# Twenty-six pairs that reorder the queues of VectorE, ScalarE and GpSimd in a two-layer hybrid encoder

## The chip, the cores and the metric

The kernel runs on one core of one Trainium2 chip. The metric is the device time of one launch in microseconds (us), as the median over several runs. Lower is better. TensorE does the matrix products, VectorE and ScalarE work on tiles in SBUF and PSUM, GpSimd works on SBUF, and SyncE's queue issues nearly all transfers.

## The reference: what is computed

Two layers, 512 grid tokens and 16 learned meta tokens, width 1024, all in float32. In short:

```python
for l in range(DEPTH):
    h = rms_norm(x, norm_g[l])
    qa, ka, va, ga, qn, kn, vn, gn, m_a, m_n = split_cols(h @ w_in[l])
    a = gqa_attention(rope(rms(qa)), rope(rms(ka)), va)      # 8 query heads, 2 key heads of 64
    b = neighbourhood_attention(rms(qn), rms(kn), vn, rpb)   # 8 heads, window 8 x 16, learned bias
    a = (a * silu(ga)) @ w_o_attn[l]
    b = (b * silu(gn)) @ w_o_na[l]
    x = x + (sigmoid(m_a) * a + sigmoid(m_n) * b) @ w_out[l]
out = rms_norm(x, final_norm_g)[:, N_META:]
```

## The kernel before, in words

Activations lie channel by channel: a tile has 128 channels as partitions and up to 528 tokens along the free axis. Every float32 product is made of three products of reduced-precision halves: `split` (line 196) writes the high half on ScalarE as a cast and the low half on VectorE as a subtraction, and a product is hi·hi, lo·hi and hi·lo (lines 327 to 329). A projection of 128 columns over 264 tokens is 24 matmuls of 128x264. Its tile is called `pp`, and in layer 0 it has two halves (`pp0_3_0`, `pp0_3_264`). For each 128x512 piece of weights, the `raw` load is followed by a cast `whi` on ScalarE (line 242) and a subtraction `wlo` on GpSimd (line 243), from rings of six buffers.

A name in an order is a tag with its layer, its head or column, and a serial number: `ptl1_2_1_2` is the low half `ptl`, layer 1, head pair 2, half 1, key tiles from 2 on.

- The grouped-query attention runs in units (layer, head pair, half): scores `S` (558, 559), an exponential into `P`, a 32x32 transpose on VectorE, a round trip through DRAM (`turn`, and the reads back at 879), the split into `pth` (ScalarE) and `ptl` (VectorE), and the sum with the values, `av` (907): two matmuls each for four key tiles, of which the ones with `ptl` can only start when the subtraction is done.
- The neighbourhood attention has, for each head, scores `Sb`, `bias` and exponentials (992, 994), transposes on TensorE into two shared PSUM banks (`ta`, `tm`, `tb`, `tc`, and `vtb`, `vtc` for the values), the splits `tah`, `tal`, `tbh`, `tbl`, `VB`, the meta part `na`, and the sum `avb` (1054).
- In layer 0 the norm of the input needs a row sum: the split `ssh`, `ssl` of the squares, and the small product `ms` (375). Beside it stand the products `mh` (474) that sum the squares of the queries and take `qh` and `ql`. `ql` is a subtraction (496) of `qs` and `qh`, which ScalarE writes when it empties a projection (492 to 494).
- The gates `zb`, `za` and `mg`, the branch outputs `oa`, `ob` with their splits, the merges `ma`, `mb`, `mx`, and a last product `pf` with the weights `wl` (1236 to 1238) fill the rest.

A scheduler puts the operations in order: it plans all engines together with costs of its own, gives split and softmax operations a higher priority, and keeps what `tc.issue_after` demands. Each engine then runs its queue strictly in order, and so does SyncE's DMA queue. So an operation that waits holds up all that stands behind it on its engine. `order only` dependencies on the same engine, as in this change, have no semaphore: they only make the scheduler put one behind the other, and it then plans all engines anew from there.

Of the kernel before, what the change touches and what calls it, by code (L numbers as in the profile page):

```python
# [58 lines left out]
BLK_PS = ((0, 0), (0, 208), (1, 0), (1, 272))  # L59

BLK_META = 448


def _window_index():
# [33 lines left out]
def trunk_kernel(ctx: ExitStack, tc: tile.TileContext, xT, w, gn, gf, bias, rope, out):  # L98
# [28 lines left out]
    def bank(pool, name, tag):  # L127
        return pool.tile([P, 512], F32, tag=tag, name=name)

    def transposed(ps, src, n=P):  # L130
        nc.tensor.transpose(ps, src, ident[:n, :n])
# [77 lines left out]
    order = []  # L209
    for l in range(DEPTH):  # L210
# [4 lines left out]
        if l == 0:  # L215

            order = order[6:]
# [238 lines left out]
    for l in range(DEPTH):  # L456
# [512 lines left out]
        def windowed_head(hd):  # L969
# [66 lines left out]
            def transposes3():  # L1036
                tp = bank(ps_t, f"tc{nm}", "tp")
                transposed(tp[:64, :P], c["bias"][:, BLK_META:BLK_META + 64])

# [115 lines left out]
        for m in range(8 + LAG_A):  # L1155
# [9 lines left out]
            if m >= LAG_A:  # L1165
# [3 lines left out]
                for a, b in merge_half(m - LAG_A, gates[m - LAG_A], WOA, oa, ma):  # L1169
                    if (end and full) or b == N:  # L1170
                        a = a if end else 0
# [52 lines left out]
    for f in range(2):  # L1224
        for t in range(4):
# [31 lines left out]
            else:  # L1257
# [6 lines left out]
                with tc.high_priority():  # L1264
# [2 lines left out]
                    nc.vector.tensor_scalar_mul(x, x, r)  # L1267
                    nc.sync.dma_start(out[P * t:P * (t + 1), 2 * h2:], x)
    side_gqa.finish()


# [45 lines left out]
```

## Time and profile before

| | |
|---|---|
| median of 3 runs | 836.88 us (836.46 to 838.2) |
| profiled execution | 837.78 us, of which the span of the trace is 834.8 us and 2.98 us lie around it |
| TensorE busy | 817.3 us, 98% of the span |
| VectorE, ScalarE, GpSimd busy | 522.5, 474.1 and 419.6 us (63, 57 and 50%) |
| chain that ended last | TensorE 81%, VectorE 6%, ScalarE 5%, DMA 4% |

The share of TensorE is so high that only the moments count in which it waits, or in which its clock is halved. The view of waits names the instruction that waits and the engine that ended the wait. In a row of the timeline the first number is the start in us from the start of the span, the second the duration, then engine, line, operation and tiles (without buffer numbers) and, in brackets, how long the engine was idle before and what ended that.

### The profile page before, as it was taken

To read this page: it belongs to the slowest core of one execution; us is meant where nothing else is said; L and a number is where in the kernel's file an instruction comes from. 1 tells how busy PE (TensorE), PEld (TensorE's weight loads), DVE (VectorE), ACT (ScalarE), POOL (GpSimd) and SP (SyncE) were. 2 spreads that over 40 slices of the span, in tenths; PEclk is the share of its full clock that TensorE was granted. 3 is DMA by queue.
4 is the path that set the end of the run, shared out by engine and by line. 5 is a ranking of instruction groups with operands and counts; after the bars stand their busy time and mean duration, and the time that the engine had idled before them with its cause. 6 is when DMAs were issued, how large, how long until landed. Compare 5 with 4: busy or idle time off the path is not lost.

```text
span 834.8 us, 16105 instructions
## 1 busy us (share of the span) xinstructions
PE 817.3 (98%) x5662; PEld 759.0 (91%) x5662; DVE 522.5 (63%) x1152; ACT 474.1 (57%) x1137; POOL 419.6 (50%) x362
## 2 busy tenths in 40 slices
PE   9899999999999999999999999999999999999997
PEld 9899999999999999999998989898898888888786
DVE  7876767677765573446448667676857755443633
ACT  8545677577865555434345457566847756443422
POOL 1654534545354444655764645453535464454751
PEclk9899999999999999999999999999999999999999
DMA  8357564766564564334655585546775555661502
GB/s 305 100 156 211 163 188 128 201 176 177 176 192 135 160 204 145 111 102 142 165 130 133 145 235 146 185 154 186 182 227 155 183 156 167 186 203 66 189 1 101
DMA packets 113248, 134.98 MB, mean 162 GB/s; under 512 B 31888, under 2 KB 66192, under 8 KB 113168
## 3 DMA queue, kind: packets, MB, share of 16 engines
q1 hardware_dynamic: 112448, 132.90, 53.6%
q8 instruction: 44, 0.72, 0.4%
q10 hardware_dynamic: 720, 1.06, 0.3%
q14 instruction: 36, 0.29, 0.1%
HBM read 98.50 MB, written 21.84 MB: 144 GB/s over the span
## 4 chain that ended last, share of the span: by engine, by line
PE 81%; DVE 6%; ACT 5%; DMA 4%; issue 2%; SPq 1%; POOLq 0%; POOL 0%; DVEq 0%; ACTq 0%
PE pp L329 17%; PE pp L327 17%; PE pp L328 17%; PE av L907 4%; PE y L329 4%; PE y L327 4%; PE y L328 4%; PE avb L1054 2%; PE S L558 2%; PE S L559 2%; PE pf L1238 2%; PE pf L1236 2%; PE pf L1237 2%; DMA turn<-P 1%; DVE ptl L196 1%
## 5 line engine op out<-in xcount | busy, mean ns | idle before, releaser
L243 POOL TENSOR_TENSOR wlo<-raw,whi 128x512 fp32r<-128x512 f32 x210 | 285.4, 1368 | 271.6 <-ACT whi L242 225.2
L327 PE MATMUL pp<-hh,whi 128*128 128x264 f32 (+3 forms) x1040 | 326.5, 314 | 0.0
L329 PE MATMUL pp<-hh,wlo 128*128 128x264 f32 (+3 forms) x1040 | 325.0, 312 | 0.0
L328 PE MATMUL pp<-hl,whi 128*128 128x264 f32 (+3 forms) x1040 | 324.2, 312 | 0.0
L329 PEld LDWEIGHTS pp<-hh,wlo 128*128 128x128 f32 x1040 | 196.7, 189 | 10.3
L328 PEld LDWEIGHTS pp<-hl,whi 128*128 128x128 f32 x1040 | 197.1, 190 | 9.3
L327 PEld LDWEIGHTS pp<-hh,whi 128*128 128x128 f32 x1040 | 196.4, 189 | 8.8
L242 ACT CAST whi<-raw 128x512 fp32r<-128x512 f32 x210 | 128.1, 619 | 133.4 <-PE pp L328 56.9
L900 POOL TENSOR_TENSOR ga<-pm,ga 32x128 fp32r<-32x128 f32 x64 | 41.2, 643 | 83.4 <-ACT ga L898 44.9
L869 DVE STREAM_TRANSPOSE P<-P 128x512 f32<-128x512 f32 x64 | 46.6, 728 | 32.3 <-ACT P L843 31.5
L196 DVE TENSOR_TENSOR ptl<-P,pth 128x512 fp32r<-128x512 f32 x64 | 56.3, 891 | 8.2 <-ACT pth L195 8.0
L1133 DVE TENSOR_TENSOR mg<-pp,rbc 128x264 f32<-128x264 f32 (+1 forms) x48 | 24.7, 514 | 47.9 <-PE pp L329 47.5
L839 DVE CUSTOM_DVE_ANT_1 P<-S,r 128x528 f32<-128x528 f32 x64 | 44.8, 700 | 13.9 <-PE S L559 12.9
L843 ACT ACTIVATE P<-P,st 128x528 f32<-128x528 f32 x64 | 47.1, 736 | 1.7
L994 ACT ACTIVATE bias<-bias,stb 128x208 f32<-128x208 f32 (+1 forms) x64 | 31.0, 486 | 22.2 <-DVE stb L992 22.1
L195 ACT CAST pth<-P 128x512 fp32r<-128x512 f32 x64 | 39.2, 613 | 2.7 <-DMA P<-turn 2.2
L1134 ACT ACTIVATE mg<-mg 128x264 f32<-128x264 f32 (+1 forms) x48 | 23.6, 492 | 27.5 <-DVE mg L1133 27.4
L907 PE MATMUL av<-ptl,VA 128*128 128x256 f32 x128 | 33.7, 291 | 3.0 <-DVE ptl L196 2.9
L328 PE MATMUL pp<-mx,whi 128*128 128x264 f32 x128 | 36.6, 286 | 0.0
L327 PE MATMUL pp<-mx,whi 128*128 128x264 f32 x128 | 36.4, 284 | 0.0
L329 PE MATMUL pp<-mx,wlo 128*128 128x264 f32 x128 | 36.3, 283 | 0.0
L907 PE MATMUL av<-pth,VA 128*128 128x256 f32 x128 | 34.2, 291 | 0.0
(534 smaller groups left out, 1704.4 us busy)
## 6 DMA issues: line engine op xcount, KB each, us to landing
raw<-in_w_dram SPq DMA_DIRECT2D x210, 256.0 KB
turn<-P SPq DMA_DIRECT2D x32, 528.0 KB
P<-turn SPq DMA_DIRECT2D x128, 128.0 KB
bias<-in_bias_dram SPq DMA_DIRECT2D x16, 480.0 KB
KB<-KB SPq DMA_DIRECT2D x24, 272.0 KB
rawl<-in_w_dram SPq DMA_DIRECT2D x16, 256.0 KB
x<-in_xT_dram SPq DMA_DIRECT2D x8, 264.0 KB
xr<-in_xT_dram SPq DMA_DIRECT2D x8, 264.0 KB
```

The costliest lines, as they stand in the source:

```text
L195: split_at["hi"] = nc.scalar.copy(hi, src)
L196: split_at["any"] = nc.vector.tensor_sub(lo, src, hi.bitcast(F32))
L242: cast = nc.scalar.copy(hi, raw)
L243: sub = nc.gpsimd.tensor_sub(lo, raw, hi.bitcast(F32))
L327: nc.tensor.matmul(ps, wh, rh[:, a:b], start=i == 0, stop=False)
L328: nc.tensor.matmul(ps, wh, rl[:, a:b], start=False, stop=False)
L329: nc.tensor.matmul(ps, wl, rh[:, a:b], start=False, stop=i == n - 1)
L839: newest["max"] = nc.vector.tensor_tensor_reduce(p[:n].rearrange("p (i k) -> p i k", i=2), S[:n, :, :HALF], scale[:n].unsqueeze(2).to_broa ...
L843: nc.scalar.activation(p[:n], p[:n], AF.Exp, bias=st[:n, 1:2], scale=1.0, accum_out=st[:n, 2:3] if total is None else total)
L869: nc.vector.transpose(c["both"][:n, a:b], c["both"][:n, a:b])
L900: nc.gpsimd.tensor_sub(tm[64 + 32 * t:96 + 32 * t, n * t:n * (t + 1)], m, tm[:32, :n].bitcast(F32))
L907: nc.tensor.matmul(c["av"], rows2(c["t"][i][0]), c["t"][i][1], start=i == 0, stop=i == 8)
```

## The change

A table of pairs and a function that is called once, after all operations are recorded. In a pair `(a, n, b, m)`, the n-th operation that writes tile `a` gets an order-only dependency on the m-th one that writes `b`, on the same engine. No operation is added, removed or changed: on all five queues the same instructions stand, in another order. One pair (`ql0_2` behind `qr0_1`) holds in the order before already.

```diff
+BEHIND = {
+    "Activation": (
...
+        ("qh0_1", 1, "whi0_5_1", 0), ("rbc0", 0, "qh0_3", 0), ("st0_7_0_0", 0, "pth0_6_0_0", 0),
+        ("whi0_14_1", 0, "qh0_3", 0), ("whi0_46_1", 0, "na0", 14), ("whi0_4_0", 0, "q0_0", 0),
...
+    "DVE": (
...
+        ("oa1_1b", 0, "bias1_6", 0), ("ob1_0", 2, "ptl1_1_0_0", 0), ("ob1_1", 2, "ptl1_2_1_2", 0), ("ql0_2", 0, "qr0_1", 1),
...
+def queue_order(tc):
+    traced, counts = {}, {}
+    for ins in tc.nc.cur_bb.bb.instructions:
+        ap = getattr(ins.outs[0], "bass_ap", None) if ins.outs else None
+        if ap is not None:
+            key = (str(ins.engine).split(".")[-1], ap.tensor.name.rpartition("_")[0])
+            traced[(*key, counts.setdefault(key, 0))] = ins
+            counts[key] += 1
+    kind = mybir.DependencyInfo(mybir.DependencyClass.NoSync, mybir.DependencyReason.DATA)
+    for engine, pairs in BEHIND.items():
+        for a, n, b, m in pairs:
+            tc.add_manual_dep(traced[engine, a, n], traced[engine, b, m].name, kind, reason="queue order")
...
     side_gqa.finish()
+    queue_order(tc)
```

Eleven pairs are ScalarE's: five of them concern the first projections (`q0_1`, `qh0_1`, `rbc0` and the casts `whi0_4_0`, `whi0_14_1`), the others put single casts, a softmax step, a gate or a part of `na0` behind `pth` or `na0`. Fourteen are VectorE's: eight put a gate, a merge, a branch output, a value split or a transpose behind a `ptl` (`mg0_34_7`, `mb0_6`, `mg0_26_3`, `ob1_0`, `ob1_1`, `mb1_3`, `VB21_2`, `Pm0_0`), the others move `P`, `VB`, `mx`, `oa` and `ql` steps. One is GpSimd's: `wl6KB` behind `gb0`.

The lines of the change are 35 higher than before (36 behind line 1304). Three places show how it moves rows.

TensorE, about 26 us into the span, where `ms` (375, now 410) takes `ssl`. Before:

```order
L474 MATMUL mh0_416<-qh0_0_421,means_r_118 10x264
L474 MATMUL mh0_416<-ql0_0_422,means_r_118 10x264
L375 MATMUL ms0_525<-means_r_118,ssh0_451 128x2
L474 MATMUL mh0_416<-qh0_1_432,means_r_118 10x264
L474 MATMUL mh0_416<-ql0_1_433,means_r_118 10x264
L375 MATMUL ms0_525<-means_r_118,ssl0_452 128x2
L375 MATMUL ms0_525<-means_r_118,ssh0_451 128x2
```

And with the change:

```order
L509 MATMUL mh0_416<-ql0_1_433,means_r_118 10x264
L509 MATMUL mh0_416<-qh0_1_432,means_r_118 10x264
L509 MATMUL mh0_416<-ql0_1_433,means_r_118 10x264
L362 MATMUL pp0_3_264_544<-hh0_0_143,whi0_3_0_259 128x264
L410 MATMUL ms0_525<-means_r_118,ssh0_451 128x2
L363 MATMUL pp0_3_264_544<-hl0_0_144,whi0_3_0_259 128x264
```
The `mh` products that need `ql0_1` now come first, and behind them twelve matmuls of `pp0_3_264` stand ahead of the first `ms` that needs `ssl`. Two of the twelve are shown.

VectorE in layer 1, about 586 us into the span, at the unit whose `ptl1_2_1_0` and `ptl1_2_1_2` are the subtractions that `av1_2_1` takes. Before:

```order
L775 TENSOR_TENSOR ob1_1_7893<-avb1_3_8356,cmb8381_8382 64x512
L196 TENSOR_TENSOR VB21_2_8369<-vtb1_2_8371,VB21_2_8369 128x6x64
L196 TENSOR_TENSOR ptl1_2_1_0_8264<-P1_2_1_8010,pth1_2_1_0_8263 128x8x2x32
L779 TENSOR_TENSOR ob1_1_7893<-ob1_1_7893,zb1_1_7607 128x512
L196 TENSOR_TENSOR ptl1_2_1_2_8325<-P1_2_1_8010,pth1_2_1_2_8324 128x8x2x32
L1112 TENSOR_TENSOR kb1_3_8390<-pp1_17_0_8403,rbc1_6354 128x64
L1113 TENSOR_TENSOR kb1_3_8390<-pp1_17_0_8403,rbc1_6354 128x200
```

And with the change:

```order
L810 TENSOR_TENSOR ob1_1_7893<-avb1_3_8356,cmb8381_8382 64x512
L231 TENSOR_TENSOR ptl1_2_1_0_8264<-P1_2_1_8010,pth1_2_1_0_8263 128x8x2x32
L231 TENSOR_TENSOR VB21_2_8369<-vtb1_2_8371,VB21_2_8369 128x6x64
L231 TENSOR_TENSOR ptl1_2_1_2_8325<-P1_2_1_8010,pth1_2_1_2_8324 128x8x2x32
L814 TENSOR_TENSOR ob1_1_7893<-ob1_1_7893,zb1_1_7607 128x512
L1147 TENSOR_TENSOR kb1_3_8390<-pp1_17_0_8403,rbc1_6354 128x64
L1148 TENSOR_TENSOR kb1_3_8390<-pp1_17_0_8403,rbc1_6354 128x200
```

Both subtractions are ahead of what filled the time: `ptl1_2_1_0` of `VB21_2`, and `ptl1_2_1_2` of the branch output `ob1_1`.

VectorE in layer 0, about 133 us into the span, in the neighbourhood heads 1 and 2. The split `VB20_1_1955<-vtb0_1` stood ten rows ahead of `tal0_2`, near the scores' step of the unit before. Before, from it on:

```order
L196 TENSOR_TENSOR VB20_1_1955<-vtb0_1_1957,VB20_1_1955 128x6x64
L775 TENSOR_TENSOR ob0_0_1390<-avb0_1_1940,cmb1977_1978 64x512
L775 TENSOR_TENSOR ob0_0_1390<-avbm0_1_1952,cmb1981_1982 64x16
L764 SCALAR_TENSOR_TENSOR za0_1_1822<-za0_1t_1823,za0_1_1822 128x528
L196 TENSOR_TENSOR ptl0_1_0_0_1964<-P0_1_0_1677,pth0_1_0_0_1963 128x8x2x32
L1112 TENSOR_TENSOR kb0_2_1990<-pp0_16_0_2003,rbc0_417 128x64
L1113 TENSOR_TENSOR kb0_2_1990<-pp0_16_0_2003,rbc0_417 128x200
L196 TENSOR_TENSOR ptl0_1_0_2_2053<-P0_1_0_1677,pth0_1_0_2_2052 128x8x2x32
L839 ISA P0_1_1_1967,st0_1_1_1_2065<-S0_1_1_1_2060,r8_0_841 128x528
L839 ISA st0_1_1_1_2065 128x1
L196 TENSOR_TENSOR tal0_2_2036<-ta0_2_2030,tah0_2_2035 128x512
```

And with the change, from `tal0_2` on:

```order
L231 TENSOR_TENSOR tal0_2_2036<-ta0_2_2030,tah0_2_2035 128x512
L904 STREAM_TRANSPOSE P0_1_1_1967<-P0_1_1_1967 128x512
L1151 TENSOR_TENSOR kb0_2_1990<-pp0_16_264_2070,rbc0_417 128x184
L1152 TENSOR_TENSOR kb0_2_1990<-pp0_16_264_2070,rbc0_417 128x64
L1154 TENSOR_TENSOR kb0_2_1990<-pp0_16_264_2070,rbc0_417 128x16 x2
L1056 CAST mm0_124<-tm0_2_2039 32x16
L231 TENSOR_TENSOR VB20_1_1955<-vtb0_1_1957,VB20_1_1955 128x6x64
L1057 TENSOR_TENSOR mm0_124<-tm0_2_2039,mm0_124 32x16
L904 STREAM_TRANSPOSE P0_1_1_1967<-P0_1_1_1967 128x544
L845 RECIPROCAL inv0_128<-suma0_0_972 128x8
L846 STREAM_TRANSPOSE inva0_0_2120<-inv0_128 128x32
L231 TENSOR_TENSOR VB20_1_1955<-vtc0_1_2043,VB20_1_1955 80x6x64
```

`VB20_1` from `vtb0_1` now stands behind `tal0_2`, a transpose of `P`, four steps of `kb0_2` and the first `mm0`, which needs the transposes `tm0_2`.

More of the change, by code (lines that the diff above doesn't have):

```diff
@@ L61 @@
 BLK_META = 448
+BEHIND = {
+    "Activation": (
[4 rows of a table added]
+    ),
+    "DVE": (
[4 rows of a table added]
+    ),
+    "Pool": (
+        ("wl6KB", 1, "gb0", 0),
+    ),
+}
+def queue_order(tc):
[10 more added lines that the diff above has]
+            tc.add_manual_dep(traced[engine, a, n], traced[engine, b, m].name, kind, reason="queue order")
 def _window_index():
```

5 rows, old and new, of the table BEHIND are left out of this document.

## The prediction

> **What bounds the kernel now.** I read the page of the profile first (busy shares, granted clock, chain), then TensorE's waits, then the granted clock in single stretches.
>
> ```profile
> PE 817.3 (98%) x5662; PEld 759.0 (91%) x5662; DVE 522.5 (63%) x1152; ACT 474.1 (57%) x1137; POOL 419.6 (50%) x362
> ...
> PEclk9899999999999999999999999999999999999999
> ...
> PE 81%; DVE 6%; ACT 5%; DMA 4%; issue 2%; SPq 1%; POOLq 0%; POOL 0%; DVEq 0%; ACTq 0%
> ```
>
> TensorE is busy for 98% of the span and carries 81% of the chain. Its work is the same in both kernels. So the change can only give or take moments in which TensorE waits, or in which its clock is low (the third slice is one: 8). These are the waits, as us in total, times, longest:
>
> ```profile
> PE av L907 <- DVE ptl L196: 2.9, 4, 1.1
> PE ms L375 <- DVE ssl L196: 2.7, 1, 2.7
> PE S L558 <- DVE stb L992: 1.7, 2, 1.0
> PE avb L1054 <- DVE na L800: 1.6, 1, 1.6
> ...
> PE vtc L741 <- DVE tal L196: 1.0, 2, 0.5
> ```
>
> VectorE ends all of them. They come to some 10 us, the most that can be won from waits. The longest costs more than itself, as TensorE's busy time and granted clock show in these stretches (start:end, length, PE busy and matmuls, ..., PEclk, DMA share, GB/s):
>
> ```profile
> 26.98:29.60 2.62, 0.00 (x1) 0.01 (x1) 2.62 (x3) 1.55 (x5) 2.00 (x2) 0.86 0.61 196
> 28.87:35.69 6.82, 6.09 (x29) 6.01 (x30) 5.27 (x11) 1.05 (x3) 2.29 (x4) 0.50 0.19 62
> 35.70:39.10 3.40, 3.40 (x30) 3.28 (x30) 2.91 (x5) 2.20 (x6) 1.89 (x3) 1.00 0.23 77
> 240.90:244.30 3.40, 1.84 (x16) 1.66 (x15) 1.87 (x5) 1.38 (x6) 2.84 (x3) 1.00 0.78 246
> ```
>
> While TensorE waits for `ssl`, the clock falls to 0.50 for 6.82 us. There 29 matmuls take 6.09 us, 0.21 each; at full clock, 30 take 3.40, 0.113 each. 29 times 0.097 is 2.8 us. This one wait therefore costs 2.6 + 2.8 = 5.4 us. The wait for `na` at 240.9 (1.6 us) leaves the clock at 1.00, so the limit lies above it; at 28.87, when the clock fell, TensorE had stood for 1.9 us.
>
> [...]
>
> **The change part by part.**
>
> *The first norm, 24 to 37 us.* These are the rows that make `ssl` late:
>
> ```profile
> 23.17 0.44 ACT L494 ACTIVATE qs<-pp 128x264 f32<-128x264 f32 x1
> 23.44 1.71 ACT L242 CAST whi<-raw 128x512 fp32r<-128x512 f32 x3
> ...
> 27.78 1.76 DVE L196 TENSOR_TENSOR ssl<-sq,ssh 128x528 fp32r<-128x528 f32 x1
> ```
>
> The pairs put those three casts ahead of the last `q0_1`, `qh0_1`, `qs0_1`. These now end 1.7 us later, at 25.3 instead of 23.6, and with them `ql0_1`, which is ahead of `ssl` on VectorE. `ssl` itself hardly moves (VectorE loses time to `ql0_1`, and wins some earlier because `whi0_4_0` no longer precedes `q0_0`): I take 30.0 instead of 29.54, with 29 and 31 as bounds, from whether the rest of its queue runs beside GpSimd as here (1.76) or not (about 0.7, as `tal` below). What does change is what TensorE has meanwhile. It takes the twelve matmuls of `pp0_3_264` (12 x 0.12 = 1.4 us) ahead of `ms`. The 2.6 us become two waits: 0.6 for `ql0_1` and 0.95 for `ssl`. Neither reaches the 1.9 us at which the clock fell, so I take it to stay at 1.00. New small waits follow, since the transposes that spread the norm now come before `pp0_4_0` (0.35), and since ScalarE has the copy `rbc0` and `whi0_14_1` behind `qh0_3` (about 1.0, as one or two evictions like the 0.44 above stand in line). 5.4 - 0.6 - 0.95 - 0.35 - 1.0 = 2.5 us gained. Bounds: 0 if the clock falls again, 5.4 if all is hidden.
>
> *Subtractions ahead of gates and outputs.* TensorE's rows at the waits, with the idle time in brackets:
>
> ```profile
> 289.27 0.28 PE L328 MATMUL pp<-hl,whi 128*128 128x264 f32 x1
> 290.27 0.39 PE L907 MATMUL av<-ptl,VA 128*128 128x256 f32 x1 [0.71 <-DVE ptl L196]
> ...
> 336.79 0.39 PE L907 MATMUL av<-ptl,VA 128*128 128x256 f32 x1 [0.46 <-DVE ptl L196]
> ...
> 538.16 0.39 PE L907 MATMUL av<-ptl,VA 128*128 128x256 f32 x1 [0.56 <-DVE ptl L196]
> ...
> 590.41 0.38 PE L907 MATMUL av<-ptl,VA 128*128 128x256 f32 x1 [1.15 <-DVE ptl L196]
> ...
> 632.94 0.39 PE L558 MATMUL S<-KA1h,Q 128*128 128x264 f32 x1 [0.99 <-DVE stb L992]
> ```
>
> From 289.27 to 290.27 are 1.00 us, where matmuls otherwise start 0.12 apart: a wait costs 0.88, the bracket and 0.17 for filling the array. And these are VectorE's instructions that stood in the way, or were slow:
>
> ```profile
> 288.14 0.43 DVE L1133 TENSOR_TENSOR mg<-pp,rbc 128x264 f32<-128x264 f32 x1 [0.86 <-PE pp L329]
> ...
> 334.92 0.43 DVE L1133 TENSOR_TENSOR mg<-pp,rbc 128x264 f32<-128x264 f32 x1 [0.93 <-PE pp L329]
> 335.27 1.46 DVE L196 TENSOR_TENSOR ptl<-P,pth 128x512 fp32r<-128x512 f32 x1
> ...
> 536.42 0.82 DVE L779 TENSOR_TENSOR ob<-ob,zb 128x512 f32<-128x512 f32 x1
> ...
> 588.59 1.77 DVE L196 TENSOR_TENSOR ptl<-P,pth 128x512 fp32r<-128x512 f32 x1
> ...
> 630.42 1.15 DVE L196 TENSOR_TENSOR oa_1b<-oa,oa_1a 128x512 fp32r<-128x512 f32 x1
> ...
> L196 DVE TENSOR_TENSOR ptl<-P,pth 128x512 fp32r<-128x512 f32 x64 | 56.3, 891 | 8.2 <-ACT pth L195 8.0
> ```
>
> At 288.14 the gate `mg0_34_7` waited 0.86 us for its projection, and `ptl0_5_1_0` behind it. Ahead of it the subtraction starts 1.2 us earlier, and all 0.88 goes. At 335 it is the same with `mg0_26_3`, which waited 0.93: the subtraction can run 1.28 earlier, and the 0.46 + 0.17 goes: 0.6. At 537 `ob1_0` goes behind `ptl1_1_0_0`, 0.75 earlier: 0.7. At 589 `ptl1_2_1_0` passes `VB21_2` and `ptl1_2_1_2` passes the 0.94 of `ob1_1`: up to 1.3, I take 1.1. At 631 the four `bias1_6` steps go ahead of `oa1_1b`, 1.08 earlier: 1.1. What comes later in turn (gates, outputs, `VB21_2`) is used many matmuls later. Sum 4.4. But a subtraction of 128x512 takes 0.68 at best (`tal`, below) and 1.77 at worst, and the mean of the 64 is 0.89. I counted 0.68. Five of them at the mean cost 5 x 0.2 = 1.0 us, so 3.4. Bounds: 1 (all five near the worst, of whose 1.1 the rows in hand hide a third) and 4.4.
>
> *`whi0_46_1` behind `na0`.* At the 1.6 us wait for `na`:
>
> ```profile
> 240.05 0.62 ACT L242 CAST whi<-raw 128x512 fp32r<-128x512 f32 x1
> 240.57 0.36 ACT L195 CAST tbh<-tb 128x256 fp32r<-128x256 f32 x1
> ...
> 241.91 0.70 DVE L800 SCALAR_TENSOR_TENSOR na<-tc,inner,na 32x128 fp32r<-32x128 f32 x2 [0.25 <-ACT na L794]
> ```
>
> Without the cast, `tbh` starts 0.5 us earlier and `na` follows. VectorE's own queue allows it, since a gate moves into idle time. ScalarE's gate between the two `na` steps stays. I take 0.4 gained of 1.6, between 0.3 and 0.5.
>
> *`VB20_1` behind `mm0`, a new wait.* At 133 us:
>
> ```profile
> 133.50 0.68 DVE L196 TENSOR_TENSOR tal<-ta,tah 128x512 fp32r<-128x512 f32 x1
> ...
> 134.33 0.50 PE L741 MATMUL vtc<-ident,vb 128*80 128x128 f32 x3 [0.52 <-DVE tal L196]
> ```
>
> Before, `vtc` waited 0.52 (0.68 with the fill) for `tal0_2`, whose bank it needs. Now `tm0_2` takes that bank and waits for `tal0_2`, which an output split of the same form as `tal` (0.68) now precedes: about 0.6 again. `vtc` then needs `VB20_1`, which stands behind four `kb0_2` steps and `mm0`: about 0.45 more. `tc0_2` needs the next `VB20_1` part, behind a transpose and two small steps: 0.4. 1.45 against 0.68 is a loss of 0.75. Bounds: 0 and 1.5.
>
> *`wl6KB` behind `gb0`.* The last products:
>
> ```profile
> 787.67 0.39 PE L1236 MATMUL pf<-wl6h,mx 128*128 128x512 f32 x1
> 787.91 0.40 PE L1237 MATMUL pf<-wl6KB,mx 128*128 128x512 f32 x1
> ...
> 788.47 0.50 PE L1236 MATMUL pf<-wl7h,mx 128*128 128x512 f32 x1
> ...
> 789.54 0.39 PE L1236 MATMUL pf<-wl0h,mx 128*128 128x512 f32 x1
> ```
>
> Three matmuls take 1.07 us where 0.24 apiece is the pace: 0.35 lost, because the last split of `mx` is late. In the new order eight matmuls of the next tile stand ahead of those two that need it, which hides 0.35 us. `wl6KB` now comes one GpSimd operation later, which the eight (8 x 0.24 = 1.9 us) cover.
>
> *The other pairs* (`Pm0_0`, `mb0_6`, `mx0_10`, `mb1_3`, `P`, three casts, the gate) stand where TensorE shows no wait in the rows above, or half a microsecond at most. I take them at 0, with 0.7 either way, as at `VB20_1`.
>
> Sum: 2.5 + 3.4 + 0.4 - 0.75 + 0.35 = 5.9 us. The profiled execution, 837.78, becomes 831.9. It lies 0.9 above the median of 836.88, for which I say 831.0.
>
> **The rivals.**
>
> *The clock falls again in the first norm.* The two new waits are 1.55 together and come close to each other. If `ssl` comes at 31, one of them is 1.9 or they add up. Then 2.8 us are lost again, and nothing is won there: 5.9 - 2.5 = 3.4 gained, 833.5. The same time comes out if the slow stretch has a cause other than the wait, since the new waits add up to about the old one. For this case speaks that 1.9 was enough; against it, that 1.6 was not. [...]
>
> *The new plan brings as many waits as it takes.* Each pair makes the scheduler plan all queues anew; at `VB20_1` that costs 0.75 by my count. Four such places (3.0), with subtractions that all meet GpSimd (2.4 more), leave 0.5: 836.4. Against it: in the other places the rows next to the pairs hardly change.
>
> *A transfer in front of the reads back: slower.* SyncE's queue now has the load `raw0_36_0` ahead of the four reads of `P0_3_0`. It needs the buffer that GpSimd frees with `wlo0_9_0`:
>
> ```profile
> 188.65 3.42 SPq L879 DMA_DIRECT2D P<-turn  x4
> ...
> 188.72 2.54 POOL L243 TENSOR_TENSOR wlo<-raw,whi 128x512 fp32r<-128x512 f32 x2 [1.18 <-issue]
> ...
> 207.47 1.17 PE av L907 x9
> ```
>
> Its first half ends at 190.0, so the reads go out 1.4 us or more later. Their sum on TensorE (the last row, from the chain) comes at 207.5, some 10 us behind the landing, so this is free as long as GpSimd is not held up. It depends on a weight load that now goes out behind the reads of the unit before. It decides once the reads are late by more than these 10 us, the gains of 5.9 and the 1.7 below. At 18 us the time is 839.
>
> **How the numbers follow.** Chances: forecast 0.58 (828 to 832.5, the upper part of gains included), clock falls again 0.27, as many waits 0.10, late transfer 0.05. 0.2% of the time, 1.7 us, is about what a measurement can tell from no change, so 835.2 is the border. Faster 0.85 (the first two), same 0.10, slower 0.05. The range goes from 827.6, where the first norm gives 4.5 and the subtractions 4.4 (a sum of 8.9 gives 828.0, and a little for the others), to 834.8, past the second case with a new wait of its size.
>
> **What would show it.** The granted clock near 29 to 36 us stays at 1.00, and `ms` waits about 1 us; `av` on `ptl` falls from 2.9 us to under 1.0, `S` on `stb` from 1.7 to 0.7, `avb` on `na` to 1.2; new are `tm` or `vtc` on `tal` and `VB`, some 1.4 us near 134. It is wrong if a stretch at 0.50 comes back anywhere, or if TensorE waits for `VB`, `KB` or `Q` tiles for over 1 us in layer 0.

## The result and the profile after

The changed kernel takes 828.89 us (median of 4 runs, 827.37 to 831.61), beside 836.67 us for the kernel before on the same chip (835.18 to 838.2). The ratio is 0.9911, with a 95% interval of 0.9893 to 0.9928: 7.8 us faster, where 5.9 were forecast. In the profiled executions the span falls from 834.8 to 827.2 us, by 7.6. The profiled times differ by more (837.78 and 829.0), because 3.0 us lay around the span in the one and 1.8 in the other; that part is no work of the kernel's.

The page of the profile after, with the busy times of the engines and the granted clock in 40 slices:

```profile
PE 814.7 (98%) x5662; PEld 758.0 (92%) x5662; DVE 516.8 (62%) x1152; ACT 474.9 (57%) x1137; POOL 417.4 (50%) x362
...
PEclk9999999999999999999999999999999999999999
```

The same 5662 matmuls are busy for 2.6 us less, and the third slice of the clock shows 9 where it showed 8. TensorE's waits after (us in total, times, longest):

```profile
PE av L942 <- DVE ptl L231: 1.3, 2, 1.0
PE ms L410 <- DVE ssl L231: 1.1, 1, 1.1
...
PE S L593 <- DVE stb L1027: 0.7, 1, 0.7
...
PE tm L166 <- DVE tal L231: 0.4, 1, 0.4
PE vtc L776 <- DVE mm L1057: 0.4, 1, 0.4
PE avb L1089 <- DVE na L835: 0.4, 1, 0.4
```

`ms` waits 1.1 us where it waited 2.7, `av` 1.3 (2.9), `S` 0.7 (1.7), `avb` 0.4 (1.6). `tm` on `tal` and `vtc` on `mm` are new. The stretch of the low clock and a part of it, in the view of busy times by stretch (length, PE, PEld, DVE, ACT and POOL busy, granted clock, DMA share, GB/s):

```profile
28.87:35.69 6.82, 5.71 (x36) 5.27 (x34) 5.89 (x11) 1.17 (x5) 3.85 (x4) 0.75 0.27 80
...
31.00:35.00 4.00, 4.00 (x22) 3.92 (x23) 3.07 (x8) 0.00 (x0) 2.66 (x3) 0.57 0.12 39
```

The mean granted clock of the first stretch is 0.75, against 0.50 before. In this execution it still fell, but for half as long: 0.57 over the four microseconds from 31 is 3.4 us at 0.50 (from 31.33 to 34.74).

Where the time came from can be read from one set of numbers: the start of a matmul in the trace after, less the start of the same matmul in the trace before. This shift is -7.38 us at the end. Its change over a stretch is what the stretch won (minus) or lost (plus):

| stretch, us | what lies there | forecast | measured |
|---|---|---|---|
| 0 to 17 | start-up; `pp` waits 0.7 for `hh` in this execution, not in most others | 0 | +0.79 |
| 17 to 44 | the first norm | -2.5 | -1.84 |
| 99 to 142 | `VB20_1` behind `mm0` | +0.75 | +0.04 |
| 166 to 191 | `vtc` waits for `mm` | | +0.41 |
| 215 to 251 | `whi0_46_1` behind `na0` | -0.4 | -1.09 |
| 288 to 300, 324 to 337 | `mg0_34_7`, `mg0_26_3` behind `ptl` | -1.5 | -0.93, -0.71 |
| 337 to 542 | `ob1_0` behind `ptl1_1_0_0` | -0.7 | +0.43 |
| 542 to 592, 592 to 641 | `VB21_2` and `ob1_1` behind `ptl`; `oa1_1b` behind `bias1_6` | -2.2 | -1.44, -1.11 |
| 738 to 799 | the last products, `wl6KB` | -0.35 | -0.55 |
| six other stretches | small shifts of both signs, among them -0.35 at 98 us, where a wait of `vtc` (0.45) is gone | 0 | -1.40 |

The five subtraction places were forecast at 4.4 together, less 1.0 for slow subtractions; they gave 3.76.

### The profile page after: what moved, and what is told of

Its sections match the earlier page's. It is cut to its first block, busy times and chain, and to the rows that moved or that the text cites. A ratio compares the mean times of both kernels' runs of the same rounds, so it can differ in the third digit from the quotient of the medians.

```text
span 827.2 us, 16100 instructions
## 1 busy us (share of the span) xinstructions
PE 814.7 (98%) x5662; PEld 758.0 (92%) x5662; DVE 516.8 (62%) x1152; ACT 474.9 (57%) x1137; POOL 417.4 (50%) x362
## 4 chain that ended last, share of the span: by engine, by line
PE 81%; DVE 5%; ACT 4%; DMA 4%; issue 3%; SPq 1%; POOL 1%; POOLq 0%; DVEq 0%; ACTq 0%
PE pp L364 17%; PE pp L362 17%; PE pp L363 17%; PE y L364 4%; PE av L942 4%; PE y L363 4%; PE y L362 4%; DMA raw<-in_w_dram 2%; PE avb L1089 2%; PE pf L1273 2%; PE pf L1271 2%; PE pf L1272 2%; PE S L593 2%; PE S L594 2%; PE pp L482 1%
```

## The experiments

All kernels keep every operation of the kernel they start from; those with "unused products" add TensorE work whose result nobody reads. Times are medians. The kernel before, run beside each group, took 836.46, 836.8, 836.02 and 836.07 us.

**The two halves of the change.** One kernel has only the five ScalarE pairs of the first norm, the other the remaining 21 pairs.

```diff
 BEHIND = {
     "Activation": (
+        ("q0_1", 1, "whi0_5_0", 0), ("qh0_1", 1, "whi0_5_1", 0), ("rbc0", 0, "qh0_3", 0),
+        ("whi0_14_1", 0, "qh0_3", 0), ("whi0_4_0", 0, "q0_0", 0),
     ),
```

> The kernel before with only five of ScalarE's pairs, those of the first norm (q0_1, qh0_1, rbc0, whi0_14_1, whi0_4_0). Theory (the gains belong to single places and add up): it gains what the changed kernel had gained between 17 and 44 us of its trace, 1.8 us, so 834.9 where the kernel before has 836.7; the clock falls for one stretch of 3.4 us instead of 6.8. Rival (the place gains nothing by itself, and what differs there is the phase of the clock from run to run): 836.7, with a stretch of 6.8 us at half clock as before.

> The changed kernel without those five pairs. Theory (places add up): 7.4 - 1.8 = 5.6 us faster than the kernel before, 831.1, and the first 45 us of the trace as before, with a stretch of 6.8 us near half clock. Rival (the pairs work through the plan as a whole): less than 4 us, over 832.7, since waits come back elsewhere.

Measured: 834.04 us, ratio 0.9979 (0.9964 to 0.9993), and 831.0, ratio 0.9938 (0.9926 to 0.995). The halves give 2.4 and 5.5 us, together 7.9 of the whole change's 7.8: as far as intervals over 2 us wide can tell, they don't disturb each other. The first norm alone gave what was forecast for it (2.5), and in its profile the clock stayed up, where one stretch at half clock had been expected:

```profile
28.87:35.69 6.82, 5.05 (x37) 4.22 (x38) 6.18 (x12) 2.04 (x8) 3.75 (x4) 1.00 0.18 65
```

The second kernel missed one point of its expectation. In its profile the clock fell for 3.41 us (a mean of 0.75 over the 6.82) and not for 6.8, and from 17 to 44 us it won 1.6 us on the kernel before, with none of the five pairs. So what a single trace shows of the clock there, the -1.84 of the table included, can't be put down to the pairs alone; the 2.4 of eight runs is the better measure.

**Is it the wait that lowers the clock?** The kernel before, with no pair, and with 19 unused products of 10x264 in the wait for `ssl` (order-only dependencies, left out below, keep them between the first two `ms`).

```diff
+                if name == "0" and t == 0 and i == 1:
+                    for _ in range(19):
+                        nc.tensor.matmul(fill[:10, :264], sel_h[0], sh[:, :264], start=True, stop=True)
                 nc.tensor.matmul(ps[:, 2 * t:2 * t + 2],
```

> The kernel before, without any of the 26 pairs, and with 19 extra products of 10x264 (2.1 us of TensorE, results unused) in the wait for ssl in the first norm. Nothing else has to change. Theory (the wait itself makes the clock fall): the granted clock stays at 1.00 from 28 to 36 us and 2.8 us are gained, 833.9. Rival (the slow stretch has a cause other than idle time): the clock falls all the same, 836.7 or up to 0.5 more.

Measured: 834.28 us, ratio 0.9968 (0.9955 to 0.9981). The row of `ms` in the timeline:

```profile
29.83 0.27 PE L411 MATMUL ms<-means_r,ssl 128*128 128x2 f32 x1 [0.55 <-DVE ssl L228]
```

And the stretch in the view of busy times:

```profile
28.87:35.69 6.82, 6.27 (x53) 5.73 (x51) 6.75 (x13) 2.71 (x7) 3.01 (x5) 1.00 0.23 69
```

`ssl` comes no earlier (`ms` starts at 29.83, before at 29.60). TensorE has merely been given something to do, and the clock stays at 1.00, where it was 0.50. Work that nobody needs wins 2.2 us, where 2.8 were expected: the wait is the cause of the low clock.

**The same for the changed kernel.** Ten unused products, written as above, ahead of the `ms` that waits.

```diff
+    row = [traced["PE", "pp0_3_264", 11]] + [traced["PE", "fill", i] for i in range(10)] + [traced["PE", "ms0", 1]]
+    for x, y in zip(row, row[1:]):
+        tc.add_manual_dep(y, x.name, kind, reason="queue order")
```

> The changed kernel with ten 10x264 products, whose result nobody reads, between the last product of the tile pp0_3 and the ms product that waits for ssl in the first norm. Theory (idle time of TensorE is what lowers the granted clock, and the changed kernel sits at the edge of it): the clock stays 1.00 in 28.87 to 35.69 us, ms on ssl falls from 1.1 us to under 0.4, and the time is 828.3 +-0.5 against 828.9, with a narrower spread than the 827.4 to 831.6 of the changed kernel's runs. Rival 1 (the ten products only delay what stands behind them): 829.5 to 830.5. Rival 2 (the clock was not what held the first norm back): 828.9, and 0.75 again in that stretch.

Measured: 828.53 us (827.92 to 829.45), ratio 0.9902 (0.9886 to 0.9918). The one row in the timeline of this stretch in which TensorE waits:

```profile
34.74 0.54 PE L621 MATMUL rb<-ident,rx 128*128 128x128 f32 x3 [1.20 <-POOL rx L243]
```

And the busy times of the stretch:

```profile
28.87:35.69 6.82, 5.53 (x44) 4.41 (x42) 6.82 (x12) 3.36 (x8) 3.41 (x4) 1.00 0.37 114
```

The clock is held, and the wait for `ssl` is gone, but `rb`, the transposes that spread the norm, now waits 1.20 us for `rx`, where it had waited 0.2 or not at all. From 29 to 41 us this kernel still gains 0.6 on the changed one, as expected. With the 0.57 that this execution was ahead since the start-up, it stands 1.16 ahead at 41 us. At the end 0.15 of it is left: the wait of `vtc` at 180 us grew from 0.4 to 1.2, and that of `avb` at 240 from 0.4 to 0.9. The theory held in its stretch; the time can't be told from the changed kernel's, and why the rest did not follow is taken up below.

**Why the place of `ob1_0` lost.** In the trace after, ScalarE's cast `whi1_20_0` had come forward there, and with it GpSimd's `wlo`. The experiment puts the cast behind ScalarE's cast of `ob1_0`.

```diff
+        ("whi1_20_0", 0, "ob1_0", 0),
```

> The changed kernel with one more pair: ScalarE's cast whi1_20_0 behind the cast of ob1_0, so that GpSimd's wlo1_20_0 comes later than the subtraction ptl1_1_0_2. Theory (that subtraction took 1.77 us because GpSimd worked beside it): it takes 0.7 us, the wait of av1_1_0 for it falls from 1.0 to under 0.2 us, and the time is 1.1 us under that of the changed kernel, 827.8. Rival (it is slow by its operands): 1.77 again, wait 1.0, 828.9.

Measured: 828.01 us, ratio 0.99 (0.9886 to 0.9913). The rows of GpSimd, VectorE and TensorE in the changed kernel's timeline:

```profile
533.36 1.39 POOL L278 TENSOR_TENSOR wlo<-raw,whi 128x512 fp32r<-128x512 f32 x1 [0.30 <-ACT whi L277]
...
533.54 1.77 DVE L231 TENSOR_TENSOR ptl<-P,pth 128x512 fp32r<-128x512 f32 x1
...
535.36 0.39 PE L942 MATMUL av<-ptl,VA 128*128 128x256 f32 x1 [1.02 <-DVE ptl L231]
```

And of VectorE and GpSimd in the experiment's:

```profile
532.78 0.68 DVE L230 TENSOR_TENSOR ptl<-P,pth 128x512 fp32r<-128x512 f32 x1
...
534.16 1.29 POOL L277 TENSOR_TENSOR wlo<-raw,whi 128x512 fp32r<-128x512 f32 x1 [1.85 <-PE av L941]
```

Beside GpSimd's subtraction VectorE's takes 1.77 us, without it 0.68. TensorE's wait goes, and the shift between 528 and 540 us improves by 1.1. The rival is refuted by these rows; the times (0.9 us apart, with intervals that overlap) would not do it. In the changed kernel GpSimd's starts first and ends at 534.75, and VectorE's ends 0.56 later. That the one is slow when the other runs beside it is what the two runs show, not why.

**ScalarE's idle time at the norm's copy.**

```diff
+        ("rbc0", 1, "qs0_3", 0),
```

> The changed kernel with the 16-wide ScalarE copy of the first norm (rbc<-rbm) queued behind the splits of q0_3, which the new plan had put behind it. Theory (ScalarE idles 5.5 us at that copy while finished q0_3 work waits behind it, and tile pp0_4_0 starts late because of it): pp0_4_0 starts 0.5 us earlier, mh on qh is gone from the waits, 828.4. Rival (the mh products come on time but the next norm step sets the start): 828.9.

Measured: 829.05 us, ratio 0.9911 (0.9897 to 0.9925): the rival, no gain. TensorE's wait for `qh` is gone, and from 29 to 41 us it wins 0.6 more than the kernel with the moved cast, whose clock was 1.00 as well. By 65 us 0.7 is lost again, most of it at 61 us, where `S` waits 0.43 for `KA0l`, and 0.4 more at 133, where `tm` waits 0.8 for `tal` (0.4). What it wins is lost downstream, as with the unused products.

**The pair that was forecast to cost 0.75.**

```diff
-    "DVE": (... ("Pm0_0", 2, "ptl0_0_1_0", 0), ("VB20_1", 0, "mm0", 4),
+    "DVE": (... ("Pm0_0", 2, "ptl0_0_1_0", 0),
```

> The changed kernel without the one pair that puts VB20_1 behind mm0. Theory from the two traces (a wait of tm on tal of 0.4 us has taken the place of one of vtc on tal of about 0.4): 828.9 +-0.4, with vtc on tal back. Rival, the prediction's step (the pair costs 0.75): 828.1.

Measured: 828.27 us, ratio 0.9902 (0.9886 to 0.9917). The time lies between the two expectations, and the intervals don't part them. The trace parts the mechanisms: at 133 us the kernel without the pair wins 0.3, and at 180 the wait of `vtc` for `mm` is gone, but `av` waits 0.4 for `ptl` at 159. It has lost 0.8 between 152 and 165, so that at 214 both are level within 0.1.

**Four mends together.**

```diff
+        ("whi1_20_0", 0, "ob1_0", 0), ("rbc0", 1, "qs0_3", 0),
+        ("vb1_2", 0, "bias1_3", 3),
+    row = ...  # ten unused products, as above
```

> The changed kernel with four mends: the ScalarE cast whi1_20 behind ob1_0 (0.9 by its own run), the 16-wide copy behind the splits of q0_3 (0.5), the ten unused products in the first norm (0.6), and the two vb1_2 steps of VectorE behind the four bias1_3 steps, for which S waits 0.7 us at 561 us (0.5). Theory (the waits are in places far apart and add up): 828.9 - 2.5 = 826.4. Rival (what is won at one wait is lost at the next, as at the place of ob1_0 in the changed kernel): no better than 828.0, that of the one mend measured.

Measured: 827.95 us, ratio 0.9895 (0.9878 to 0.9913): the rival. The casts and `vb1_2` gave what they should (1.1 at 535, 0.36 at 561: `S` waits 0.4 for 0.7). The half microsecond of the first norm was again lost at 180 us, where TensorE lost 0.8 against the changed kernel. There ScalarE shows what holds it, and TensorE pays 8 us later:

```profile
172.74 0.62 ACT L280 CAST whi<-raw 128x512 fp32r<-128x512 f32 x1 [3.31 <-DMA raw<-in_w_dram]
...
180.66 0.50 PE L783 MATMUL vtc<-ident,vb 128*80 128x128 f32 x3 [1.12 <-DVE mm L1064]
```

The cast waits 3.31 us for a load of weights, `raw0_21_1`. SyncE's queue (`SPq`) says why. In the kernel before:

```profile
158.85 1.78 SPq L237 DMA_DIRECT2D raw<-in_w_dram  x3
...
170.00 0.33 SPq L872 DMA_DIRECT2D turn<-P  x1
```

And in the changed kernel:

```profile
168.07 0.34 SPq L907 DMA_DIRECT2D turn<-P  x1
168.45 1.77 SPq L272 DMA_DIRECT2D raw<-in_w_dram  x3
...
172.62 0.62 ACT L277 CAST whi<-raw 128x512 fp32r<-128x512 f32 x1 [2.25 <-PE av L942]
```

Before, `raw0_21_1` was one of the three loads at 158.85. Now it is the first of those behind the write `turn0_2_1`, 9 us later; counted in order, the load after it moved behind the write too (168.99 for 160.15). They move only in the kernels with the `VB20_1` pair; without that pair `raw0_21_1` goes out at 158.3. The pair names VectorE alone, but the plan made for it moved a load on SyncE. In the changed kernel the load lands at 172.54 and the cast follows at 172.62. The row names TensorE's `av`, which ended at 172.50, but the kernel of the next experiment starts the same cast 2 us before its `av` ends, so the load is what it waits for. Whatever brings TensorE there earlier waits for it.

**The load put back.**

```diff
+    "SP": (
+        ("turn0_2_1", 0, "raw0_21_1", 0), ("raw0_9_0", 0, "pm0_2_1", 0), ("bias0_5", 0, "raw0_9_0", 0),
+    ),
```

The last two pairs keep the loads behind it in their places. One kernel has this and the four mends, a second the same without the unused products.

> The changed kernel with the four mends, and on SyncE's queue the weight load raw0_21_1 ahead of the write of P0_2_1 to memory, not behind it; nothing else moves. Theory (from 168 us on ScalarE and VectorE stand at the same time however early TensorE comes, because ScalarE's cast waits for that load, which shares the transfer engines with the write; so what the first norm gives is lost again at 180 us): the load goes out some 3 us earlier, into a stretch in which the transfer engines are idle, ScalarE's cast waits under 1 us instead of 3.3, vtc on mm falls from 1.1 to 0.4 us, and the time from 827.95 to 827.2. Rival (the transfer engines are full from 168 to 180 us either way, and the reads of P0_2_1 or the next load become what is late): 827.95, with the wait at 180 us as before under another name.

> The same without the ten unused products in the first norm. Theory (the products hold the clock at 1.00, but in their place rb waits 1.2 us for rx where ms had waited 1.1 for ssl): within 0.4 of the filled one, 827.2, if the clock stays at 1.00, as in the run with the norm copy moved; 828.2 if it falls. Rival (the products are themselves in the way): 826.6.

Measured: 826.09 us (825.26 to 826.75), ratio 0.9879 (0.9862 to 0.9897), and 826.84, ratio 0.9888 (0.9868 to 0.9908). Between the first and the changed kernel (0.9893 to 0.9928) the intervals barely touch. Against the four mends alone (0.9878 to 0.9913) they overlap widely, so what the load by itself is worth has to be read from the trace. In its queue the load stands at 160.76, the write where it was, and the cast no longer waits for a transfer:

```profile
160.76 0.43 SPq L278 DMA_DIRECT2D raw<-in_w_dram  x1
166.96 0.33 SPq L917 DMA_DIRECT2D turn<-P  x1
...
169.28 0.62 ACT L283 CAST whi<-raw 128x512 fp32r<-128x512 f32 x1
```

`vtc` has no wait left at 180 us, and the shift there improves by 1.2. At 240 us 0.75 of this is given back, where `avb` waits 1.1 for `na`. Without the unused products the clock fell again in the profile (0.75 as the mean of 28.87 to 35.69, against 1.00), and the time is 0.75 longer, near the 1.0 expected for that case. The traces don't put this down to the clock: from 29 to 41 us the two stay level within 0.05, since the filled kernel waits 1.20 for `rx` there, and the 0.5 by which they differ there arose in the start-up.

**The next wall, and the pair at it.** At 240 us ScalarE's split of `P0_4_0` waits 1.20 us for the reads back. One kernel puts two loads behind those reads. The other is the changed kernel without the pair of `whi0_46_1`; only that cast moves.

```diff
+        ("raw0_39_0", 0, "pm0_4_0", 0),
```

```diff
-        ("whi0_46_1", 0, "na0", 14),
```

> The kernel with the four mends and raw0_21_1 moved forward, and on SyncE's queue the two loads raw0_39 behind the reads back of P0_4_0 (and with them the two raw0_40 behind the sums, as the new plan has it). Theory (at 240 us it is again transfers that hold ScalarE: its split of P0_4_0 waits 1.2 us for the reads back, which go out only when the write is done, and the write shares the engines with the two loads): the reads go out up to 1.5 us earlier, the split waits under 0.4, avb on na falls from 1.1 to under 0.5 us, and the time from 826.1 to 825.5. Rival 1 (the loads are then late for their casts): a wait of TensorE for whi or wlo of 1 us or more near 244 to 256 us, 827 or more. Rival 2 (the write itself takes as long alone): 826.1.

> The changed kernel without the one pair that puts the cast whi0_46_1 behind na0 on ScalarE; nothing else moves on any engine. The prediction's step: the pair is worth 0.4, so avb on na is 0.4 longer than with it and the time 829.3. Rival (by the shift of TensorE between the two traces at this place): it is worth 1.1, 830.0. Second rival (the wait there has been 0.4 to 1.2 in kernels with the pair, since it is set by when TensorE comes and not by the cast): no difference, 828.9.

Measured: 826.03 us, ratio 0.9885 (0.9868 to 0.9902), and 829.65 (827.87 to 833.43), ratio 0.9934 (0.9912 to 0.9956). The first is half a hit: the split waits 0.83 instead of 1.20, `avb` 0.7 instead of 1.1, TensorE comes 0.4 earlier, and no load is late, but the time can't be told from the 826.09 without it. For the second the times leave the size open. The timeline gives it, from ScalarE's split `pth` to TensorE's `avb`. In the changed kernel:

```profile
237.54 0.61 ACT L230 CAST pth<-P 128x512 fp32r<-128x512 f32 x1
...
240.24 0.36 PE L1089 MATMUL avb<-na,VB 128*128 128x256 f32 x1 [0.35 <-DVE na L835]
```

And without the pair:

```profile
236.03 0.60 ACT L229 CAST pth<-P 128x512 fp32r<-128x512 f32 x1
...
239.25 0.36 PE L1088 MATMUL avb<-na,VB 128*128 128x256 f32 x1 [0.97 <-DVE na L834]
```

From the split to `avb` are 2.70 us with the pair and 3.22 without, and so it is in every trace: 2.69 or 2.70 in the ten with the pair, 3.21 or 3.22 in the four without. The pair is worth 0.52 where the wait is long enough. The rest of what was won there in the changed kernel belongs to how early TensorE comes and when the reads are back: this split starts 2.00 us earlier than in the kernel before, where TensorE comes 1.39 earlier.

## Why the prediction was right, and where not

The time (831.0 forecast, 828.89 measured) lies in the range and in the likeliest case; the change won 1.9 us more than the sum. That it came so near is in part luck: by the table, places fell short of the forecast by 1.9 us together, and others won 3.4 more than it.

- **The first norm: right in mechanism, with a condition that failed.** Forecast 2.5, measured 2.4 by itself and 1.84 in the profiled execution. `ssl` was put at 30.0 with a wait of 0.95; `ms` started at 30.60 after 1.11. The step that failed is "neither reaches the 1.9 us at which the clock fell". The stretch at 0.50 that the prediction had named as a sign of being wrong came back. Of seven profiles with the new order here and no unused products the clock fell in three, the changed kernel's among them, and stayed up in four, though the wait was 1.1 or 1.2 in all. So the length of the wait alone does not decide, and what else does was not shown. Between the changed kernel and the one with the cast moved, where it stayed up, lie 1.1 us in this stretch. In the five profiles with unused products, one of them of the kernel before, it stayed at 1.00. So the rival "the clock falls again" took place in some executions, at a price of 1.1 us and not 2.5.
- **The five subtractions: right in sum (3.4 forecast, 3.76), wrong in one place.** At 289 and 336 us the wait went as worked out (0.93 and 0.71 for 0.88 and 0.6). At 589 and 631 it was 1.44 and 1.11 for 1.1 and 1.1. At 537 the forecast 0.7 became a loss of 0.43: the subtraction stood where it was meant to, but the new plan had brought GpSimd's beside it, and 1.77 us is the worst case that the prediction had named. The allowance of 1.0 was the right size, though it was one subtraction that cost it, not five. The 0.17 added to the brackets is what the rows leave: 1.00 us between two starts, less the 0.12 between starts elsewhere and the bracket of 0.71. That it goes into filling the array, no run shows.
- **`whi0_46_1`: right in size.** Forecast 0.4 (0.3 to 0.5), shown 0.52. The stretch gave 1.09; the rest is the arrival of ScalarE's split.
- **`VB20_1`: the step failed.** The waits forecast for `vtc` and `tc0_2` at 134 us are not there; `tm` waits 0.37, where `vtc` had waited 0.52. The pair's price came 46 us later and by another queue: `vtc` on `mm`, 0.4 in the changed kernel and up to 1.2 where TensorE comes earlier, and gone in the kernels with the load put back. Without the pair the trace loses as much elsewhere, so that its net price is not shown. The prediction followed VectorE's queue for this pair and did not look for a load that it moves on SyncE's. The rival on transfers had the right kind of cause but the wrong load.
- **`wl6KB`: right.** 0.55 for 0.35; around 787 us the products stand 0.23 apart without a gap.
- **The other pairs: 1.4 won where 0 (0.7 either way) was taken.** One of the waits listed before stood there, `vtc` on `tal` at 98 us, which gave 0.35; the rest lies where no wait was listed. Which of the pairs did it was not tried. This and the 0.7 more at `na0` are the largest terms that the sum lacked. Against them stand the 0.8 lost at the start and the 0.7 missing in the first norm, both in the profiled execution.

## What to carry to other kernels

On a kernel whose busiest engine is at 98%, look for moments in which it stands or runs at half clock, not for busy time to remove; a wait that lowers the clock costs twice (here 2.7 us of wait, and a clock of 0.50 for 6.82 us), and filling it with work that nobody needs won 2.2 us. Whether a wait of 1.1 or 1.2 us lowered the clock differed between profiles (it did in three of seven), so one trace is not enough to judge it. When a pair of operations is reordered under a scheduler, compare all queues, the transfers' above all: one load that the plan moved behind a write took back what the mends ahead of it had won, until it was put back. A gain that vanishes downstream is found by asking which engine stands at the same time in both traces although TensorE comes earlier.

## What the runs showed of the hardware that was not expected

- The granted clock fell after a wait of 1.1 us, with small products of 128x2 behind it, in three profiles of seven, and stayed at 1.00 in the other four, where the wait was 1.1 or 1.2 us and the same products stood behind it. The three are those of the changed kernel, of the one without the `VB20_1` pair and of the unfilled one with the load put back. In the changed kernel the clock is 1.00 from 4.02 to 31.33 us, 0.50 for 3.41 us, and 1.00 from 34.74 to 826.6. These are 3.4 us with the wait and the 3.4 us behind them, in the changed kernel and in the one with the cast moved (the granted clock is the third number from the right):

```profile
27.91:31.33 3.42, 2.31 (x21) 2.09 (x19) 3.26 (x4) 2.03 (x6) 1.45 (x2) 1.00 0.58 183
31.33:34.74 3.41, 3.41 (x17) 3.33 (x18) 2.65 (x7) 0.00 (x0) 2.40 (x3) 0.50 0.07 21
```

```profile
27.45:30.87 3.42, 2.31 (x20) 2.07 (x18) 3.42 (x5) 2.31 (x7) 1.74 (x2) 1.00 0.63 192
30.87:34.28 3.41, 3.19 (x27) 2.83 (x27) 2.77 (x8) 0.00 (x0) 2.41 (x3) 1.00 0.11 35
```

TensorE is busy for 2.31 us in both, and the clock behind is 0.50 in the one and 1.00 in the other. Nor do the lengths of the waits put them in order: in the kernel before, the clock fell in the wait of 2.7 us, to 0.50 for 6.82 us, but stayed at 1.00 after the one of 1.56 us at 242 us, which is longer than the 1.1 after which it fell. With the load put back the filled kernel stayed at 1.00, and the unfilled one was at 0.50 from 31.5 us on, for about 3.4 us. What decides was not shown.

- The kernels with the wait filled seem to vary less: 0.9 to 1.5 us between the lowest and highest run in the four made from the changed one, 1.3 to 5.6 in the six unfilled ones with the new order of the first norm besides it. With 4 to 8 runs each this is a hint. The granted clock points the same way: it was 0.998 or 0.999, as a mean over the execution, in all 25 runs of the five filled kernels, and between 0.993 and 0.999 in those of the kernel before.
